# Weight halves by accumulating and casting DMA in the two gated MLPs of a hybrid decoder trunk

## The chip, the cores and the metric

The kernel runs on one core of a Trainium2 chip, written against the engines directly with a tile framework that orders each engine's instructions when the program is built. The metric is device time in microseconds of one launch. The kernel before takes 1498.43 us, the median of three runs (1496.72 to 1500.53).

## The reference, cut to what matters

Two layers over 528 tokens (16 learned ones and 512 of the sequence), model width 1024. Layer 0 is forgetting attention with 16 heads, layer 1 a gated linear recurrence with 8 heads; each is followed by the MLP that the change touches, with 2816 hidden columns:

```python
def conv_ffn(h, norm_g, w_gate, w_up, conv_w, conv_b, w_down):
    xn = rms_norm(h, norm_g)
    a = xn @ w_gate
    a_pad = jnp.pad(a, ((0, 0), (CONV_WIDTH - 1, 0), (0, 0)))
    a = (conv_b + conv_w[0] * a_pad[:, 0:L] + conv_w[1] * a_pad[:, 1:L + 1]
         + conv_w[2] * a_pad[:, 2:L + 2])
    return (jax.nn.silu(a) * (xn @ w_up)) @ w_down
```

All inputs and outputs are float32.

## The kernel before, in words

Activations lie transposed: 128 features by 528 tokens per tile, 8 such tiles for the width, 22 for the hidden columns. Products in float32 are built from three passes of TensorE in its reduced format (F32R). Each operand is split into hi, the value rounded to that format, and lo, what is left over; a product is hi·hi + hi·lo + lo·hi (`proj_unit`, L204, L207, L208). So every weight tile has to be split before use, and that is what `weights` does (L174 to L194), from three pools: `raw` with 2 buffers, `hi` and `lo` with 3 each. A tile is 128 x 1024 numbers (512 KB) or 128 x 896 (448 KB).

1. SyncE's queue issues the load of `raw` from HBM (L189). It can start when a raw buffer is free, that is when the split two tiles back has read it.
2. ScalarE casts `raw` to `hi` (L190), when TensorE has given up the hi buffer of three tiles back.
3. VectorE subtracts: `lo = raw - hi` (L191, recorded at the helper's line L122).

The run has six parts in a row: attention, first MLP (from 388 to 776 us of the profile), recurrence, and second MLP (from 1118 us to the end) are the four large ones, with output projections ahead of each MLP. An MLP (`ffn`) first writes the split activations `xhi`, `xlo` and the norm's factors `rsb`. Then it goes through the 22 hidden tiles m, called turns in what follows. A turn takes a gate weight tile, 24 matmuls for each half of the tokens, evicted by VectorE into `A` (L1048); the convolution of width three (L1050, L1053, L1056); a sigmoid on ScalarE (L1057); the up weight tile with its matmuls, multiplied in as they are evicted (L1062); and the split of the result into `ahi` (ScalarE, L1063) and `alo` (VectorE). In the first MLP GpSimd clears two columns of `A` each turn (L1046); the second starts at a later token and needs none. The down part then takes, for each of 8 output tiles, three weight tiles of 1024, 896 and 896 columns (22 blocks of 128), and VectorE adds the sum to the residual `h` (L1070). In the first MLP the tokens of a product go in two halves of 264 (`halves`, since 528 is more than a bank's 512): `unit` takes all weight tiles that it is given for the first half, then the same for the second. For gate and up that is one weight tile, used 24 + 24 times in a row. In the down part it is the three tiles of an output tile, one after the other, and then the same three again. In the second MLP the gate has two halves of 256 and 258 tokens, up and down one pass of 512.

Matmul sums go to the PSUM banks in rotation; the MLPs use six of them (`psp` 2, `pss` 4). The framework writes out the order of each engine at build time; each engine takes its own list strictly in that order, and waits at an instruction until what it needs is there.

Of the kernel before, what the change touches and what calls it, by code (L numbers as in the profile page):

```python
# [12 lines left out]
F32 = mybir.dt.float32  # L13
# [3 lines left out]
AF = mybir.ActivationFunctionType  # L17
ALU = mybir.AluOpType
# [3 lines left out]
P = 128  # L22
D = 1024
KT = D // P
# [50 lines left out]
def halves(t0):  # L75

    n = (T - t0) // 4 * 2
    return [(t0, n), (t0 + n, T - t0 - n)]


class Builder:
# [89 lines left out]
    def vcol(self, i):  # L171
        return self.vec[:, i : i + 1]

    def weights(self, src, n, w=P, parts=1):  # L174

        nc = self.nc
        raw = self.wraw.tile([P, 8 * P], F32, name="raw", tag="raw")[:, : n * w]
        hi = self.whi.tile([P, 8 * P], F32R, name="hi", tag="hi")[:, : n * w]
        lo = self.wlo.tile([P, 8 * P], F32R, name="lo", tag="lo")[:, : n * w]

        def load(c):
            nc.sync.dma_start(raw[:, c], src[:, c])
            nc.scalar.copy(hi[:, c], raw[:, c])
            self.sub(lo[:, c], raw[:, c], hi[:, c].bitcast(F32))

        self.raw = raw
        u = hi.rearrange("p (k c) -> p k c", c=w), lo.rearrange("p (k c) -> p k c", c=w), n
        if parts == 1:
            nc.sync.dma_start(raw, src)  # L189
            nc.scalar.copy(hi, raw)  # L190
            self.sub(lo, raw, hi.bitcast(F32))  # L191
            return u
        m = n * w // parts
        return *u, [partial(load, slice(i * m, i * m + m)) for i in range(parts)]  # L194
# [514 lines left out]
    def attend(self, o0, o1, p, ds, v, po, s2, maskk):  # L709
# [32 lines left out]
        for j in range(last + 1):  # L742
            w = []
            for hd in range(2):
                w.append(weights(hd, j))
                yield 0.25
            if due:
                values(due)
                yield 0.35 * len(due)
                due = []  # L750
            ready.append((j, w))
            if len(ready) == 2:
                due, ready = ready, []
# [265 lines left out]
    def ffn(self, ctx, layer, a0, o0):  # L1019

        nc, a = self.nc, self.a
        ga, up = (halves(t0) if T - t0 > 512 else [(t0, T - t0)] for t0 in (a0, o0))
        gcol, cw, cb = ((V_FFN0, V_CW0, V_CB0), (V_FFN1, V_CW1, V_CB1))[layer]
        sp = self.pool(f"ffn1_{layer}", 1, ctx=ctx)
        s2 = self.pool(f"ffn2_{layer}", 2, ctx=ctx)
        self.normsplit(gcol, a0)
        segs = (SEG0, SEG1)[layer]
        am, rs = self.token_stats(segs)
        self.spread_rs(rs, segs)
        def unit(w, toks, x):  # L1030
            for t0, tn in toks:
                ps = self.anybank()[:, :tn]
                for _ in self.proj_unit(ps, w, x, t0, tn):
                    pass
                yield ps, t0, tn

        ahi = sp.tile([P, NF, T - o0], F32R, name="ahi")
        alo = sp.tile([P, NF, T - o0], F32R, name="alo")
        ax = [(ahi[:, k, :], alo[:, k, :]) for k in range(NF)]
        n = T - o0  # L1040
        for m in range(NF):
            A = s2.tile([P, T + 2], F32, name="A", tag="A")
            t = s2.tile([P, T], F32, name="t", tag="t")
            s = s2.tile([P, T], F32, name="s", tag="sg")
            if o0 == 0:
                nc.gpsimd.memset(A[:, 0:2], 0.0)  # L1046
            for ps, t0, tn in unit([self.weights(a[f"gu{layer}"][m, 0], KT)], ga, self.x):
                nc.vector.tensor_tensor(A[:, 2 + t0 : 2 + t0 + tn], ps, self.rsb[:, t0 : t0 + tn], ALU.mult)  # L1048
            c0 = cw + 3 * m
            nc.vector.tensor_scalar(  # L1050
                t[:, :n], A[:, o0 + 2 : T + 2], self.vcol(c0 + 2), self.vcol(cb + m), ALU.mult, ALU.add
            )
            nc.vector.scalar_tensor_tensor(  # L1053
                t[:, :n], A[:, o0 + 1 : T + 1], self.vcol(c0 + 1), t[:, :n], ALU.mult, ALU.add
            )
            nc.vector.scalar_tensor_tensor(t[:, :n], A[:, o0:T], self.vcol(c0), t[:, :n], ALU.mult, ALU.add)  # L1056
            self.act(s[:, :n], t[:, :n], AF.Sigmoid)  # L1057
            nc.vector.tensor_tensor(t[:, :n], t[:, :n], s[:, :n], ALU.mult)
            nc.vector.tensor_tensor(t[:, :n], t[:, :n], self.rsb[:, o0:], ALU.mult)
            for ps, t0, tn in unit([self.weights(a[f"gu{layer}"][m, 1], KT)], up, self.x):  # L1060
                tv = t[:, t0 - o0 : t0 - o0 + tn]
                nc.vector.tensor_tensor(tv, ps, tv, ALU.mult)  # L1062
            nc.scalar.copy(ahi[:, m, :], t[:, :n])  # L1063
            self.sub(alo[:, m, :], t[:, :n], ahi[:, m, :].bitcast(F32))
        dn = [(t0 - o0, tn) for t0, tn in up]
        for m in range(KT):
            us = [self.weights(a[f"dn{layer}"][m][:, b * P : e * P], e - b) for b, e in ((0, 8), (8, 15), (15, 22))]
            for ps, t0, tn in unit(us, dn, ax):
                hv = self.h[:, m, o0 + t0 : o0 + t0 + tn]
                nc.vector.tensor_tensor(hv, ps, hv, ALU.add)  # L1070
                if layer == 1:
                    nc.sync.dma_start(a["out"][m][:, t0 : t0 + tn], hv)
            if layer == 0:
                self.sumsq(m)
# [99 lines left out]
```

## Time and profile before

| what | value |
|---|---|
| median of 3 runs | 1498.43 us (1496.72 to 1500.53) |
| profiled execution | 1497.61 us, span of its instructions 1495.8 us |
| TensorE (PE) busy | 1474.4 us, 99% |
| VectorE (DVE) busy | 892.8 us, 60% |
| ScalarE (ACT) busy | 524.9 us, 35% |
| GpSimd (POOL) busy | 32.3 us, 2% |
| HBM read | 116.10 MB |
| DMA queue q1 (issued by SyncE) | 131.57 MB, 29.1% of the 16 DMA engines' span |
| granted TensorE clock | 0.998 |

In the profile PE is TensorE, PEld its weight loads, DVE is VectorE, ACT ScalarE, POOL GpSimd, SP SyncE, and SPq the queue of DMAs that SyncE issues. `L190` is line 190 of the kernel. A matmul's record is longer than the distance to the next one, because matmuls are pipelined; time is read from distances and stretches, not from single matmuls.

### The profile page before, as it was taken

What the parts mean: (1) busy time and instruction counts of PE and PEld (TensorE: products, weight loads), DVE (VectorE), ACT (ScalarE), POOL (GpSimd) and SP (SyncE); (2) the same over time, 40 slices, a digit from 0 to 9 for tenths busy, and PEclk for the clock granted to TensorE, in tenths of its full rate; (3) what the DMA queues carried; (4) which work ended last, traced back from release to release, by engine and by line L of the source; (5) the groups of instructions that cost most, each with busy time, mean ns of one, the idle gap of its engine ahead of it and who ended that gap; (6) DMA issues with size and microseconds to landing.
All of it is one profiled execution on the core that took longest, in us unless ns stands there. A gap on an engine that the chain in (4) does not pass through costs nothing.

```text
span 1495.8 us, 27540 instructions
## 1 busy us (share of the span) xinstructions
PE 1474.4 (99%) x11352; PEld 1361.8 (91%) x11352; DVE 892.8 (60%) x1881; ACT 524.9 (35%) x1007; POOL 32.3 (2%) x113
## 2 busy tenths in 40 slices
PE   7999999999999999999999999999999999999999
PEld 6888888979999999999999989999999989988887
DVE  6555555775677667643335667676566667675221
ACT  5456555654233222222222333333342232222121
POOL 6000000000000000000000000000000000000000
PEclk9999999999999999999999999999999999999999
DMA  4433344413232322322322211211132232332331
GB/s 156 117 103 88 102 106 127 116 52 96 96 99 85 96 88 88 95 78 80 104 83 71 72 35 52 71 63 52 57 101 97 86 99 87 96 98 83 121 104 60
DMA packets 44821, 133.33 MB, mean 89 GB/s; under 512 B 7432, under 2 KB 7944, under 8 KB 44696
## 3 DMA queue, kind: packets, MB, share of 16 engines
q1 hardware_dynamic: 44696, 131.57, 29.1%
q8 instruction: 89, 1.46, 0.4%
q14 instruction: 36, 0.29, 0.1%
HBM read 116.10 MB, written 2.10 MB: 79 GB/s over the span
## 4 chain that ended last, share of the span: by engine, by line
PE 96%; DMA 2%; DVE 1%; SPq 1%; ACT 1%; issue 0%; DVEq 0%; ACTq 0%
PE pss L208 13%; PE pss L207 13%; PE pss L204 13%; PE psp L204 12%; PE psp L207 12%; PE psp L208 12%; PE psp L253 5%; PE psc L737 2%; PE pss L888 1%; PE pss L666 1%; PE pss L722 1%; PE pss L867 1%; PE pss L723 1%; DMA h<-h 1%; PE pss L963 1%; PE pss L894 1%
## 5 line engine op out<-in xcount | busy, mean ns | idle before, releaser
L190 ACT CAST hi<-raw 128x1024 fp32r<-128x1024 f32 (+2 forms) x218 | 221.8, 1018 | 569.4 <-PE pss L207 235.3
L122 DVE TENSOR_TENSOR lo<-raw,hi 128x1024 fp32r<-128x1024 f32 (+2 forms) x222 | 262.8, 1185 | 148.7 <-ACT hi L190 143.5
L204 PE MATMUL psp<-xhi,hi 128*128 128x264 f32 (+2 forms) x1160 | 332.9, 288 | 6.5 <-ACT xhi L273 6.5
L207 PE MATMUL psp<-xlo,hi 128*128 128x264 f32 (+2 forms) x1160 | 333.6, 288 | 3.4 <-DVE xlo L274 3.4
L208 PE MATMUL psp<-xhi,lo 128*128 128x264 f32 (+2 forms) x1160 | 332.7, 287 | 0.0
L208 PE MATMUL pss<-xhi,lo 128*128 128x264 f32 (+2 forms) x824 | 253.7, 308 | 0.0
L207 PE MATMUL pss<-xlo,hi 128*128 128x264 f32 (+2 forms) x824 | 253.0, 307 | 0.0
L204 PE MATMUL pss<-xhi,hi 128*128 128x264 f32 (+2 forms) x824 | 252.9, 307 | 0.0
L204 PEld LDWEIGHTS psp<-xhi,hi 128*128 128x128 f32 x1160 | 219.1, 189 | 11.1 <-ACT xhi L273 6.5
L207 PEld LDWEIGHTS psp<-xlo,hi 128*128 128x128 f32 x1160 | 219.5, 189 | 7.7 <-DVE xlo L274 4.1
L208 PEld LDWEIGHTS psp<-xhi,lo 128*128 128x128 f32 x1160 | 219.5, 189 | 1.2 <-issue 1.0
L204 PEld LDWEIGHTS pss<-xhi,hi 128*128 128x128 f32 x824 | 155.2, 188 | 7.8
L207 PEld LDWEIGHTS pss<-xlo,hi 128*128 128x128 f32 x824 | 155.0, 188 | 7.9
L208 PEld LDWEIGHTS pss<-xhi,lo 128*128 128x128 f32 x824 | 155.0, 188 | 7.7
L207 PE MATMUL pss<-alo,hi 128*128 128x264 f32 (+1 forms) x330 | 106.1, 322 | 0.0
L208 PE MATMUL pss<-ahi,lo 128*128 128x264 f32 (+1 forms) x330 | 106.0, 321 | 0.0
L204 PE MATMUL pss<-ahi,hi 128*128 128x264 f32 (+1 forms) x330 | 105.9, 321 | 0.0
L115 ACT ACTIVATE s<-t 128x528 f32<-128x528 f32 (+1 forms) x44 | 28.1, 639 | 121.6 <-DVE t L1056 121.6
L253 PE MATMUL psp<-hi,xhi 128*128 128x256 f32 x232 | 67.4, 290 | 2.7 <-ACT v L540 2.7
L208 PEld LDWEIGHTS pss<-ahi,lo 128*128 128x128 f32 x330 | 62.3, 189 | 4.9
L204 PEld LDWEIGHTS pss<-ahi,hi 128*128 128x128 f32 x330 | 62.1, 188 | 4.9
L253 PE MATMUL psp<-lo,xhi 128*128 128x256 f32 x232 | 66.5, 287 | 0.0
(405 smaller groups left out, 2603.3 us busy)
## 6 DMA issues: line engine op xcount, KB each, us to landing
raw<-gu SPq DMA_DIRECT2D x88, 512.0 KB
raw<-dn SPq DMA_DIRECT2D x32, 448.0 KB
pk<-stg SPq DMA_DIRECT2D x48, 264.0 KB
raw<-dn SPq DMA_DIRECT2D x16, 512.0 KB
raw<-wqk SPq DMA_DIRECT2D x14, 512.0 KB
raw<-wv SPq DMA_DIRECT2D x8, 512.0 KB
raw<-wg SPq DMA_DIRECT2D x8, 512.0 KB
raw<-hv SPq DMA_DIRECT2D x8, 512.0 KB
```

The lines of the kernel that those rows point to most:

```text
L115: ins = self.nc.scalar.activation(out, in_, func, **kw)
L122: self.nc.vector.tensor_tensor(out, x, y, ALU.subtract)
L190: nc.scalar.copy(hi, raw)
L204: ins = mm(ps, hi[:, i, :], xh, start=k == 0, stop=False)
L207: mm(ps, hi[:, i, :], xl, start=False, stop=False)
L208: mm(ps, lo[:, i, :], xh, start=False, stop=k == total - 1)
L253: mm(ps[:tn, :256], y[:, t0 : t0 + tn], w, start=n == 0, stop=n == 23)
L666: mm(o, q1[0:66, qs : qs + qn], k1[0:66, c0:c1], start=True, stop=False)
L722: self.score = mm(o, k1[0:98, ks : ks + kn], q1[0:98, q0:o1], start=True, stop=False)
L723: mm(o, k2[:, ks : ks + kn], q2[:, q0:o1], start=False, stop=True)
L737: ins = mm(o, v[:kn, j, 2 * (p % 2) + hd, :], w[hd][0], start=j == 0, stop=j == last)
L867: mm(pl[:, i, :, :], kp[:, t0 : t0 + tn], qk[:, t0 // 2 : (t0 + tn) // 2, :], start=True, stop=True)
```

## The change

`weights` gets a parameter `form`, set in `ffn` by the layer and by no other caller.

In the first MLP (`add`) ScalarE casts raw to hi as before, then writes `lo = -hi` with a second pass, and a transfer issued by GpSimd adds raw onto lo in SBUF (`accum_op=ALU.add`). VectorE's subtraction is gone there. The raw buffer is now read by that transfer, so it is free when the transfer has landed.

In the second MLP (`cast`) a transfer issued by GpSimd writes hi straight from HBM, converting float32 to F32R on the way; ScalarE's cast is gone there. Raw is still loaded from HBM by SyncE's queue, and VectorE still subtracts.

```diff
-    def weights(self, src, n, w=P, parts=1):
+    def weights(self, src, n, w=P, parts=1, form=None):
...
         if parts == 1:
             nc.sync.dma_start(raw, src)
-            nc.scalar.copy(hi, raw)
-            self.sub(lo, raw, hi.bitcast(F32))
+            if form == "cast":
+                nc.gpsimd.dma_start(hi, src)
+            else:
+                nc.scalar.copy(hi, raw)
+            if form == "add":
+                nc.scalar.activation(lo, hi.bitcast(F32), AF.Copy, scale=-1.0)
+                nc.gpsimd.dma_start(lo, raw, accum_op=ALU.add)
+            else:
+                self.sub(lo, raw, hi.bitcast(F32))
             return u
...
     def ffn(self, ctx, layer, a0, o0):
+        form = ("add", "cast")[layer]
...
-            for ps, t0, tn in unit([self.weights(a[f"gu{layer}"][m, 0], KT)], ga, self.x):
+            for ps, t0, tn in unit([self.weights(a[f"gu{layer}"][m, 0], KT, form=form)], ga, self.x):
...
-            for ps, t0, tn in unit([self.weights(a[f"gu{layer}"][m, 1], KT)], up, self.x):
+            for ps, t0, tn in unit([self.weights(a[f"gu{layer}"][m, 1], KT, form=form)], up, self.x):
...
-            us = [self.weights(a[f"dn{layer}"][m][:, b * P : e * P], e - b) for b, e in ((0, 8), (8, 15), (15, 22))]
+            us = [self.weights(a[f"dn{layer}"][m][:, b * P : e * P], e - b, form=form) for b, e in ((0, 8), (8, 15), (15, 22))]
```

The lines of the changed kernel are numbered anew: `weights` by up to seven more (the casting transfer is L192, the cast L194, the negation L196, the accumulating transfer L197), `ffn` by nine more.

ScalarE in the middle of the first MLP, before. The numbers behind the names tell buffers apart; each `hi` is one weight tile, gate and up in turn, and `s` is the sigmoid.

```order
L190 CAST hi_6156<-raw_6155 128x1024
L115 ACTIVATE s_5961<-t_5960 128x528
L190 CAST hi_6220<-raw_6219 128x1024
L1063 CAST ahi_5188<-t_5960 128x528
L190 CAST hi_6284<-raw_6283 128x1024
L115 ACTIVATE s_6089<-t_6088 128x528
```

The same place in the changed kernel:

```order
L115 ACTIVATE s_5973<-t_5972 128x528
L194 CAST hi_6236<-raw_6235 128x1024
L1072 CAST ahi_5188<-t_5972 128x528
L196 ACTIVATE lo_6237<-hi_6236 128x1024
L194 CAST hi_6301<-raw_6300 128x1024
L196 ACTIVATE lo_6302<-hi_6301 128x1024
```

Each cast into hi has got a negation behind it. For the tile whose cast comes after the sigmoid, a gate tile, `ahi` of the turn stands between the cast and its negation; for the other, an up tile, nothing does.

ScalarE in the down part of the first MLP, before: three weight tiles of an output tile, with the square and the split `xhi` for the next layer's norm.

```order
L190 CAST hi_8321<-raw_8320 128x1024
L190 CAST hi_8327<-raw_8326 128x896
L190 CAST hi_8333<-raw_8332 128x896
L266 ACTIVATE sq_8317<-h_58 128x528
L273 ACTIVATE xhi_100<-h_58,vec_59 128x528
```

and in the changed kernel:

```order
L194 CAST hi_8371<-raw_8370 128x1024
L196 ACTIVATE lo_8372<-hi_8371 128x1024
L194 CAST hi_8378<-raw_8377 128x896
L196 ACTIVATE lo_8379<-hi_8378 128x896
L274 ACTIVATE sq_8367<-h_58 128x528
L281 ACTIVATE xhi_100<-h_58,vec_59 128x528
L194 CAST hi_8385<-raw_8384 128x896
L196 ACTIVATE lo_8386<-hi_8385 128x896
```

Each cast has its negation right behind it, and the third tile now comes after the square and `xhi` instead of ahead of them.

GpSimd in the turns of the first MLP, before, did nothing but clear A:

```order
L1046 MEMSET A_6087 128x2
L1046 MEMSET A_6215 128x2
L1046 MEMSET A_6343 128x2
L1046 MEMSET A_6471 128x2
L1046 MEMSET A_6599 128x2
```

and in the changed kernel:

```order
L1055 MEMSET A_6231 128x2
L197 DMA lo_6237<-raw_6235 128x1024
L197 DMA lo_6302<-raw_6300 128x1024
L1055 MEMSET A_6361 128x2
L197 DMA lo_6367<-raw_6365 128x1024
L197 DMA lo_6432<-raw_6430 128x1024
```

Two accumulating transfers now stand between two clearings of A, one for a gate and one for an up tile.

GpSimd in the second MLP, where it had nothing to do before, now issues the casting transfers one behind the other:

```order
L192 DMA hi_13385<-gu1 128x1024
L192 DMA hi_13449<-gu1 128x1024
L192 DMA hi_13486<-gu1 128x1024
L192 DMA hi_13550<-gu1 128x1024
L192 DMA hi_13587<-gu1 128x1024
```

Nothing else stands on GpSimd's list from there to the end. SyncE's list of loads is the same in both kernels but for the line numbers. On TensorE a few matmuls of the norms' factors stand some places earlier at the start of each MLP; otherwise its order is the same but for the banks that some sums go to.

## Prediction

> **What bounds the kernel now.** I read the page first (busy shares, chain), then a table of stretches for the four parts of the two MLPs, then the waits and the order of time inside one turn of the first MLP, and last the DMA traffic in windows of a microsecond or so.
>
> ```profile
> span 1495.8 us, 27540 instructions
> PE 1474.4 (99%) x11352; PEld 1361.8 (91%) x11352; DVE 892.8 (60%) x1881; ACT 524.9 (35%) x1007; POOL 32.3 (2%) x113
> PE 96%; DMA 2%; DVE 1%; SPq 1%; ACT 1%; issue 0%; DVEq 0%; ACTq 0%
> ...
> 388.00:646.00 258.00, 258.00 (x2126) 258.00 (x2125) 179.32 (x278) 74.62 (x90) 2.12 (x22) 1.00 0.28 89
> 646.00:776.00 130.00, 130.00 (x1064) 130.00 (x1063) 44.89 (x57) 33.55 (x40) 0.00 (x0) 1.00 0.28 84
> 1124.00:1372.00 248.00, 248.00 (x1569) 224.06 (x1569) 174.10 (x256) 73.59 (x88) 0.00 (x0) 1.00 0.29 91
> 1372.00:1496.00 124.00, 120.21 (x518) 97.11 (x516) 29.43 (x30) 20.54 (x21) 0.00 (x0) 1.00 0.31 95
> ```
>
> The four long rows are stretches (length, then busy time of PE, PEld, DVE, ACT, POOL, then granted clock, DMA share, GB/s): gate and up of the first MLP, its down part, and the same two of the second. In three of them TensorE is busy for the whole stretch; in the fourth it lacks only the kernel's end. The clock is at 1.00. So taking work from VectorE or ScalarE, both far from full here, can give nothing. The change can only lose, and it loses where a weight tile comes later than TensorE wants it. The question is how much time a tile has.
>
> A turn of the first MLP is two weight tiles, gate and up:
>
> ```profile
> 501.27 1.05 ACT L190 CAST hi<-raw 128x1024 fp32r<-128x1024 f32 x1 [4.17 <-PE psp L207]
> 507.10 1.05 ACT L190 CAST hi<-raw 128x1024 fp32r<-128x1024 f32 x1 [1.36 <-PE pss L207]
> 508.13 0.64 ACT L1063 CAST ahi<-t 128x528 fp32r<-128x528 f32 x1
> 512.93 1.05 ACT L190 CAST hi<-raw 128x1024 fp32r<-128x1024 f32 x1 [4.16 <-PE pss L207]
> ...
> 501.81 0.55 DVE L1050 TENSOR_SCALAR t<-A,vec 128x528 f32<-128x528 f32 x1
> 502.35 1.23 DVE L122 TENSOR_TENSOR lo<-raw,hi 128x1024 fp32r<-128x1024 f32 x1
> ...
> 503.60 6.16 SPq L189 DMA_DIRECT2D raw<-gu  x2
> ...
> SPq L189 <- DVE lo L122: 212.2, 39, 7.4
> ACT hi L190 <- PE pss L207: 72.0, 28, 4.6
> ACT hi L190 <- PE psp L207: 31.6, 13, 4.2
> ```
>
> The turn is 512.93 - 501.27 = 11.66 us, a tile 5.83. The last three rows are waits between 400 and 640 us (who <- for whom: us in total, times, longest). There the cast into hi waits for TensorE to give up the buffer three tiles back (28 + 13 = 41 casts in 240 us, one per 5.83), not for its load. The load of the next but one raw tile waits for the subtraction (39 times, 212.2 us, 5.4 each of the 5.83). So the loop that can close is the one through the two raw buffers: load, split, and only then the load two tiles on. It must fit into one turn.
>
> ```profile
> 503.60:504.50 0.90, 0.90 (x10) 0.90 (x9) 0.86 (x2) 0.00 (x0) 0.00 (x0) 1.00 0.00 0
> 504.50:506.50 2.00, 2.00 (x19) 2.00 (x18) 1.27 (x2) 0.64 (x1) 0.10 (x1) 1.00 0.83 252
> 506.50:507.40 0.90, 0.90 (x10) 0.90 (x9) 0.78 (x2) 0.30 (x1) 0.00 (x0) 1.00 0.12 41
> ...
> 47.35 3.66 DMA raw<-wqk
> 51.03 1.05 ACT hi L190
> ...
> raw<-gu SPq DMA_DIRECT2D x88, 512.0 KB
> raw<-wqk SPq DMA_DIRECT2D x14, 512.0 KB
> raw<-dn SPq DMA_DIRECT2D x32, 448.0 KB
> ```
>
> The load issued at 503.60 moves nothing for 0.9 us, then traffic runs until about 507.4; where a load of that size stands on the chain of waits (third block), it counts 3.66 us and the cast follows at once. Today's loop of gate and up is 3.66 + 1.05 + 1.23 = 5.9 of 11.66 us: half the turn is spare.
>
> The down part of the first MLP is tighter, by its order of work: the three weight tiles of an output tile are gone through for the first half of the tokens and then all three again for the second, so each holds its hi and lo buffers until its second pass, and there are three buffers. One output tile there:
>
> ```profile
> 706.55 1.05 ACT L190 CAST hi<-raw 128x1024 fp32r<-128x1024 f32 x1 [7.61 <-PE pss L207]
> 709.15 0.94 ACT L190 CAST hi<-raw 128x896 fp32r<-128x896 f32 x1 [1.55 <-PE pss L207]
> 712.40 0.94 ACT L190 CAST hi<-raw 128x896 fp32r<-128x896 f32 x1 [2.31 <-DMA raw<-dn]
> 713.24 0.64 ACT L266 ACTIVATE sq<-h 128x528 f32<-128x528 f32 x1
> ...
> 722.71 1.05 ACT L190 CAST hi<-raw 128x1024 fp32r<-128x1024 f32 x1 [8.20 <-PE psp L207]
> ...
> 707.63 1.23 DVE L122 TENSOR_TENSOR lo<-raw,hi 128x1024 fp32r<-128x1024 f32 x1 [3.53 <-ACT hi L190]
> ```
>
> It takes 722.71 - 706.55 = 16.16 us, 0.367 for each of its 2 x 22 weight blocks. The third cast already waits for its load: the raw buffer came free with the subtraction of the first tile, at 708.86, and the cast follows 3.54 us later. So here both loops run in one: raw of the third tile hangs on the split of the first, and the split of the next first tile on TensorE's passage through the third.
>
> **The change, part by part: first MLP.** Removed: 68 subtractions on VectorE (1.23 us for 1024 columns), worth nothing since it has idle time there. Added on ScalarE: 68 passes lo = -hi. The trace has no such pass of 1024; by
>
> ```profile
> L273 ACT ACTIVATE xhi<-h,vec x32: 710/724/736, 5.7 to 1119.6; 128x528 fp32r<-128x528 f32 x24, 128x514 fp32r<-128x514 f32 x8
> ```
>
> a pass with a factor takes 0.72 against the 0.64 of ahi, a cast of the same 528 elements, so 0.08 more: 1.05 + 0.08 = 1.13 us for 1024, and 0.94 + 0.07 = 1.01 for 896. 68 of them, some 75 us, come to an engine that now works 108 of 388 us: no bound by themselves. But each stands in its tile's loop, and in ScalarE's new order the cast ahi (0.64) stands between the cast and the negation of each gate tile.
>
> Added on GpSimd: 68 accumulating transfers, lo += raw. Let La be the time from the end of the negation until one of 512 KB has landed. Raw is free only then, as the transfer reads it. GpSimd's memsets of A, which stand between, wait only for the convolution two turns back, and add nothing.
>
> No accumulating transfer is in the trace. From below, it is a load of the same size: 3.66. From above, every byte is read twice and written once in turn, 1.57 MB, at the rate of the nearest SBUF-to-SBUF traffic:
>
> ```profile
> 285.50 6.12 SPq L551 DMA_DIRECT2D pk<-stg  x6
> ...
> 287.50:290.50 3.00, 3.00 (x27) 2.94 (x26) 2.65 (x5) 1.15 (x6) 0.00 (x0) 1.00 0.98 199
> ```
>
> 199 GB/s with the DMA engines full (0.98): 7.9 us and the 0.9 ahead of it, 8.8. I take the middle case, two reads with the write alongside: 1.05 MB / 199 = 5.3, with 0.9 before, La = 6.2, and 0.9 + 0.92 / 199 = 5.5 for 448 KB. It is nearest to that row, the only one without the HBM in it. For being delayed by other transfers I add nothing: the HBM load reached 252 GB/s at a share of 0.83, so full engines with whole weight rows move more than 199, and that margin stands for the delay. Its bound is the load's own 0.28 x 5.83 = 1.6 us for each transfer in a loop.
>
> The Trainium skill ("DMA: Bandwidth & Descriptors", section "SDMA does more than copy") lists the add in a transfer as an elementwise reduction of two streams, which speaks for two reads; no run here shows it.
>
> Gate and up: the loop of a gate tile becomes 3.66 (load) + 1.05 (hi) + 0.64 (ahi) + 1.13 (-hi) + La = 6.48 + La against 11.66. Up to La = 5.18 it costs nothing; with 6.2 the turn is 12.68, 1.02 more. Of 22 turns one and a half run on tiles loaded ahead: 20.5 x 1.02 = 21 us.
>
> Down: the loop over one output tile is the third tile's load 3.54, cast 0.94, negation 1.01 and transfer 5.5; TensorE's first pass through it 7 x 0.367 = 2.57 and the second pass through the first tile 8 x 0.367 = 2.94; and then the next first tile's cast 1.05, negation 1.13 and transfer 6.2. Sum 24.9 us against 16.16, 8.7 more, seven times from one output tile to the next: 61 us. This loop is 13.3 + 1.875 La, so it is full at La = 1.5 already; at 3.66 it is 20.15, and the part loses 4.0 x 7 = 28 us. Only here does every reasonable La cost something.
>
> **Second MLP.** ScalarE loses 68 casts, worth nothing with TensorE full. The raw load stays, so the weights are read from HBM twice, once through the casting transfer on GpSimd's queue. That waits for TensorE to free hi; behind it stand only other such transfers. It lands between 3.66 us after issue (a load) and 6.6 (the 2.9 us of traffic from 504.5 to 507.4 doubled by the raw load beside it). VectorE's subtraction waits for it, so evictions queue behind that; but six PSUM banks of at least 248 / 88 = 2.8 us each stand between them and TensorE. The tile is ready at worst 6.6 + 0.77 (one VectorE operation in the way) + 1.23 = 8.6 us after the buffer came free. All tokens go in one pass in up and down there, so no tile is held for a second one, and the next use is two tiles on: 2 x 248 / 44 = 11.3, in the down part 2 x 120.2 / 24 = 10.0. Hidden: I take 0, with 1.4 us to spare. DMA share goes from 0.29 to some 0.6.
>
> The few matmuls of the norms that change place at the two MLPs' starts stay between others while TensorE has work: 0.
>
> **Sum.** 21 + 61 = +82 us. The profiled execution took 1497.61 (span 1495.8), 0.8 under the median 1498.43; 1498.4 + 82 = 1580 us. All of it hangs on La: around 6.2, each microsecond is 20.5 + 1.875 x 7 = 34 us. Low end, La 3.66: 0 + 28, 1526 us. High end, La 8.8 and 1.6 of delay on each transfer: a turn of 18.5, 6.8 over, x 20.5 = 140; an output tile of 29.8 + 4.9 = 34.7, 18.5 over, x 7 = 130; 1768 us.
>
> **Rivals.** (a) Not slower: raw, or the sum, is there within 1.5 us of the negation, 1498 us. Place: the down part's loop; it decides at La = 1.5, where 13.3 + 1.875 La passes 16.16. For it: gate and up have half a turn spare, and TensorE is never idle there now. Against: a plain load of this size moves nothing for 0.9 us and takes 3.66. Chance 0.05.
>
> (b) As quick as a load: the engines read both streams at once, La 3.7 to 4.5; gate and up hidden, the down part +28 to +40, 1526 to 1540 us. For it: loads use the engines to 0.28 only. Against: an add must read what it adds to. Chance 0.18.
>
> The Trainium skill's fit for a GpSimd transfer ("DMA: Bandwidth & Descriptors", "Anatomy of one DMA") is 2.0 us plus bytes over 436 GB/s, an estimate of 3.2 us here; by it the sum would be 3.1 x 7 = +22 us in the down part alone. The trace's plain load, at 3.66, is already longer than that.
>
> (c) Much slower: three passes, or transfers in each other's way; DMA share near 1 in the first MLP, over 1640 up to 1768 us. For it: 0.98 at only 199 GB/s in the SBUF-to-SBUF row. Against: the load's 252 at 0.83. Chance 0.17.
>
> (d) The second MLP pays too: the casting transfer needs over about 9 us (8.0 in the down part). At 10, 1 x 20.5 + 2 x 12 = +45 us on top, 1625 us. Against: HBM loads land in 3.66. Chance 0.03.
>
> (e) Faster: only if matmuls themselves ran closer together, for which no row speaks. 0.02. That the casting transfer does not replace the raw load is certain from the code; it alters no term.
>
> One rule would add to mine: the Trainium skill ("SBUF — State Buffer", "Who interferes with whom") says that VectorE in a two-port mode keeps GpSimd from writing a transfer's descriptors, and tensor_scalar is of a kind named there. By that rule, at most the 0.55 us of L1050 above would come on top of each turn, an estimate of 11 us in all; no run here shows it.
>
> **How the numbers follow.** My case, La 4.5 to 7.5, 1540 to 1640 us, 0.55; (a) 0.05; (b) 0.18; (c) 0.17; (d) 0.03; (e) 0.02. About 0.3% (4.5 us) is what a measurement of this kernel can tell from no change. Slower is 0.55 + 0.18 + 0.17 + 0.03 = 0.93, same 0.05, faster 0.02. The range runs from 1520, which takes (b) in, to 1690, above which lies about half of (c); below it lie (a) and (e).
>
> **What would show it.** Right: in the first MLP ScalarE's cast waits for the raw load instead of TensorE, SP's queue waits for the accumulating transfer, TensorE has gaps ahead of matmuls that read lo, most of them in the down part, where an output tile takes about 25 us; a turn of gate and up takes about 12.7; the second MLP keeps 248 and 124 us. The step that carries the sum is La = 6.2: a turn still at 11.66 with a slower down part makes (b) right, a turn of 15 or more (c). Gaps in the second MLP would make (d) right; a down part still at 130 us would overturn my loop.

## The result and the profile after

The changed kernel takes 1542.30 us (median of three runs, 1537.16 to 1542.36) against 1498.43 us: 1.0281 times as long, 95% interval 1.0251 to 1.0311, so 44 us slower. The forecast was 1580 us with a range of 1520 to 1690: right in sign, inside the range, 38 us too high. The profiled execution took 1542.36 us, with a span of 1540.6.

First the head of the page after: span, busy engines, shares of the chain that ended last.

```profile
span 1540.6 us, 27729 instructions
PE 1489.8 (97%) x11352; PEld 1370.2 (89%) x11352; DVE 817.5 (53%) x1813; ACT 520.4 (34%) x1007; POOL 129.0 (8%) x249
PE 70%; DMA 19%; issue 5%; ACT 4%; SPq 1%; DVE 1%; POOL 0%; POOLq 0%; ACTq 0%; DVEq 0%
```

TensorE was 96% of that chain and is 70% now, with transfers at 19%. The span grew by 44.8 us and TensorE's busy time by 15.4 for the same 11352 matmuls; the other 29 are idle time. The waits of the whole trace (who <- for whom: us in total, times, longest) say for what:

```profile
PE pss L216 <- DMA lo<-raw: 17.7, 17, 2.2
PE psp L216 <- DMA lo<-raw: 10.7, 10, 2.7
ACT hi L194 <- DMA raw<-gu: 131.5, 29, 7.4
```

TensorE's 17.7 + 10.7 = 28.4 us are all ahead of matmuls that read lo, waiting for the accumulating transfer. ScalarE's cast, which waited for TensorE before, now waits for the raw load, and in the waits of SyncE's own queue the load waits for the accumulating transfer, once for each of the 68 tiles:

```profile
SPq L190 <- DMA lo<-raw: 408.0, 68, 11.4
```

The parts' limits are read from three rows in each trace's order of time: the first matmul of the gate, the first one of the down part, and the first operation of the recurrence's gates. Before, then after:

```profile
388.02 0.29 PE L204 MATMUL pss<-xhi,hi 128*128 128x264 f32 x1
...
646.98 0.28 PE L204 MATMUL psp<-ahi,hi 128*128 128x264 f32 x1
...
776.90 0.13 DVE L787 TENSOR_TENSOR mx<-vec 128x8 f32<-128x8 f32 x1
```

```profile
391.05 0.29 PE L212 MATMUL pss<-xhi,hi 128*128 128x264 f32 x1
...
669.34 0.28 PE L212 MATMUL psp<-ahi,hi 128*128 128x264 f32 x1
...
821.85 0.13 DVE L795 TENSOR_TENSOR mx<-vec 128x8 f32<-128x8 f32 x1
```

Gate and up take 669.34 - 391.05 = 278.3 us instead of 259.0: 19.3 lost. The down part takes 152.5 instead of 129.9: 22.6. Together 41.9 of the 44.8. The other 3.0 were lost ahead of the gate's first matmul (391.05 against 388.02); three runs below whose time is that of the kernel before lost 1.1, 2.1 and 2.9 us there too, so they are no sign of the change. The table of stretches for the second MLP, 44 us later than in the prediction (columns as there), has the time and TensorE's share of before; ScalarE's busy time fell from 73.6 and 20.5 us, and the DMA share rose from 0.29 and 0.31:

```profile
1168.00:1416.00 248.00, 248.00 (x1569) 224.16 (x1570) 174.41 (x254) 26.93 (x43) 23.25 (x44) 1.00 0.57 182
1416.00:1540.00 124.00, 120.92 (x521) 97.75 (x519) 31.92 (x33) 0.62 (x1) 11.08 (x21) 1.00 0.59 183
```

In the middle of gate and up, the chain of waits in order of time (start, length, what) is a closed ring of two transfers and ScalarE:

```profile
529.09 4.55 DMA lo<-raw
...
533.69 4.55 DMA raw<-gu
...
538.31 2.83 issue
...
541.16 4.56 DMA lo<-raw
```

This turn is 541.16 - 529.09 = 12.07 us, against 11.66 before, and it is one of the shortest. Between the casts of these two gate tiles lie 17 turns, 12.86 us on average (12.0 to 15.3):

```profile
431.37 1.05 ACT L194 CAST hi<-raw 128x1024 fp32r<-128x1024 f32 x1 [3.96 <-DMA raw<-gu]
...
649.91 1.05 ACT L194 CAST hi<-raw 128x1024 fp32r<-128x1024 f32 x1 [6.10 <-DMA raw<-gu]
```

The 2.83 called issue are ScalarE's cast, `ahi` and negation, which the next rows show in the order of its time, up to the 0.28 between the negation's end and the transfer:

```profile
538.32 1.05 ACT L194 CAST hi<-raw 128x1024 fp32r<-128x1024 f32 x1 [6.05 <-DMA raw<-gu]
539.27 0.63 ACT L1072 CAST ahi<-t 128x528 fp32r<-128x528 f32 x1
539.80 1.05 ACT L196 ACTIVATE lo<-hi 128x1024 fp32r<-128x1024 f32 x1
```

In the quoted turn La is 0.28 + 4.55 = 4.8 us. Over all 68, issue to landing is longer:

```profile
DMA to landing us min/median/max: 4.2/5.7/8.3
```

**A correction.** The part on the change says that TensorE's order is otherwise the same but for banks. That is wrong for the down part of the first MLP. Let A, B, C be an output tile's three weight tiles and 1, 2 the two halves of the tokens; counted in blocks of 128 at the matmuls that read lo, TensorE's list for the second output tile is:

```
before:  A1 x8   B1 x7   C1 x7   A2 x8   B2 x7   C2 x7
after:   A1 x8   A2 x4   B1 x7   A2 x4   B2 x7   C1 x7   C2 x7
```

When the framework wrote out the order for the changed kernel, it mixed the two halves, so a tile's hi and lo buffers are given up much earlier. The mix is not the same for every output tile: from the third on, C1 stands between two parts of B2. One of the experiments puts the order of before back.

### The profile page after: what moved, and what is told of

It is laid out like the page before. It is cut to its first block, busy times and chain, and to the rows that moved or that the text cites. A ratio compares the mean times of both kernels' runs of the same rounds, so it can differ in the third digit from the quotient of the medians.

```text
span 1540.6 us, 27729 instructions
## 1 busy us (share of the span) xinstructions
PE 1489.8 (97%) x11352; PEld 1370.2 (89%) x11352; DVE 817.5 (53%) x1813; ACT 520.4 (34%) x1007; POOL 129.0 (8%) x249
## 4 chain that ended last, share of the span: by engine, by line
PE 70%; DMA 19%; issue 5%; ACT 4%; SPq 1%; DVE 1%; POOL 0%; POOLq 0%; ACTq 0%; DVEq 0%
PE psp L212 9%; PE psp L215 9%; PE psp L216 9%; DMA lo<-raw 8%; DMA raw<-gu 8%; PE pss L216 8%; PE pss L215 7%; PE pss L212 7%; PE psp L261 5%; PE psc L745 2%; DMA raw<-dn 2%; ACT lo L196 2%; PE pss L896 1%; ACT hi L194 1%; PE pss L730 1%
## 5 line engine op out<-in xcount | busy, mean ns | idle before, releaser
L194 ACT CAST hi<-raw 128x1024 fp32r<-128x1024 f32 (+2 forms) x150 | 151.9, 1014 | 400.6 <-DMA raw<-gu 131.5
L122 DVE TENSOR_TENSOR lo<-raw,hi 128x1024 fp32r<-128x1024 f32 (+2 forms) x154 | 181.7, 1182 | 159.3 <-DMA hi<-dn 59.2
L216 PEld LDWEIGHTS pss<-xhi,lo 128*128 128x128 f32 x824 | 155.8, 189 | 18.1 <-DMA lo<-raw 10.4
L197 POOL DMA_DIRECT2D lo<-raw x68 | 59.5, 875 | 444.2 <-ACT lo L196 343.1
L122 DVE TENSOR_TENSOR alo<-t,ahi 128x528 fp32r<-128x528 f32 (+1 forms) x44 | 30.8, 700 | 117.2 <-ACT ahi L1072 117.2
L196 ACT ACTIVATE lo<-hi 128x1024 fp32r<-128x1024 f32 (+1 forms) x68 | 70.2, 1033 | 1.4
```

The costliest lines, as they stand in the source:

```text
L122: self.nc.vector.tensor_tensor(out, x, y, ALU.subtract)
L196: nc.scalar.activation(lo, hi.bitcast(F32), AF.Copy, scale=-1.0)
L197: nc.gpsimd.dma_start(lo, raw, accum_op=ALU.add)
L216: mm(ps, lo[:, i, :], xh, start=False, stop=k == total - 1)
```

## The experiments

Each is the changed kernel with one edit, run beside the kernel before on the same chip (medians of before 1498.05, 1498.27 and 1498.45 us). Losses of gate and up, and of the down part, are read from the same three rows as above, in the profiled execution, which can lie some us off the median.

**The two parts of the change, each alone.** First the accumulating form in the first MLP only:

```diff
-        form = ("add", "cast")[layer]
+        form = ("add", None)[layer]
```

> The first MLP as in the changed kernel, the second as before. Theory L (the loop through the two raw buffers of the first MLP - load, cast, negation, accumulating transfer, next load - sets the time there, and the casting transfers of the second MLP are hidden): 1537 to 1543 us, the whole loss. Rival C (the casting transfers take part of the loss, by queueing or by DMA traffic): less than 1530.

Measured: 1541.14 us, ratio 1.0291 (1.0275 to 1.0307): the changed kernel's loss. Then the casting form in the second MLP only:

```diff
-        form = ("add", "cast")[layer]
+        form = (None, "cast")[layer]
```

> The first MLP as before, the second as in the changed kernel. Theory L: the same as the kernel before, 1496 to 1501 us, ratio within 0.997 to 1.003. Rival C: 1505 us or more, with TensorE gaps in the second MLP.

Measured: 1498.38 us, ratio 1.0003 (0.9994 to 1.0012). The casting transfer is hidden, and the whole loss is the first MLP's.

**A third raw buffer** in the first MLP, every third tile from a pool of its own:

```diff
-        raw = self.wraw.tile(
+        third = form == "add" and self.nadd % 3 == 2
+        self.nadd += form == "add"
+        raw = (self.wraw3 if third else self.wraw).tile(
```

> The changed kernel with a third raw buffer in the first MLP (two from the old pool and one from a pool of its own), so that a load waits for the accumulating transfer three tiles back instead of two. The same bytes are moved. Theory L: three tiles are there for a loop of some 12 us where 17.5 are needed by TensorE, so gate and up fall back to 11.66 us a turn and the total to 1498 to 1508 us (in the down part the hi and lo buffers may still leave some). Rival B (bandwidth: the DMA engines, at a share of 0.7 in the first MLP, are what is short): no change, 1535 to 1545 us.

Measured: 1505.69 us, ratio 1.0052 (1.0032 to 1.0072). The stretches of gate and up and of the down part with what follows:

```profile
388.00:660.00 272.00, 271.45 (x2234) 271.11 (x2233) 134.96 (x238) 120.95 (x137) 41.87 (x68) 1.00 0.78 180
660.00:840.00 180.00, 174.27 (x1411) 168.32 (x1410) 51.23 (x124) 67.52 (x83) 19.79 (x33) 1.00 0.57 140
```

TensorE is full in the first, at a higher DMA share (0.78) than the 0.71 which the changed kernel has between 388 and 669 us. The transfers are no shorter (4.2/5.9/8.0), so it is neither their length nor their traffic that costs time there, but that the loop runs through two raw buffers. Gate and up lose nothing (258.9 us) where they lost 19.3, the down part 8.1 instead of 22.6. The order of the down part is mixed here nearly as in the changed kernel (from the second output tile on C1 comes after one or two blocks of B2 there).

**TensorE's order of before** forced in the down part of the first MLP: the first matmul of each half waits in the list for the last one of the half before.

```diff
-                mm(ps, lo[:, i, :], xh, start=False, stop=k == total - 1)
+                self.endmm = mm(ps, lo[:, i, :], xh, start=False, stop=k == total - 1)
...
-        def unit(w, toks, x):
+        def unit(w, toks, x, chain=False):
...
-                for _ in self.proj_unit(ps, w, x, t0, tn):
+                for _ in self.proj_unit(ps, w, x, t0, tn, self.endmm if chain else None):
...
-            for ps, t0, tn in unit(us, dn, ax):
+            for ps, t0, tn in unit(us, dn, ax, layer == 0):
```

> The changed kernel with TensorE's order in the down part of the first MLP as the kernel before had it: all three weight tiles for the first half of the tokens, then all three for the second. Theory O (the prediction's loop over an output tile was right for that order, and the built program got around it by mixing the two halves): the down part costs 13.3 + 1.875 La with La of 4.9 to 5.8, that is 22.5 to 24.2 us an output tile instead of 18.5, 7 x 4 to 5.7 more, total 1566 to 1582 us. Rival R (the raw buffers' loop alone sets the down part, whatever TensorE's order): 1537 to 1545 us.

Measured: 1590.62 us, ratio 1.0618 (1.059 to 1.0645): 48 us more than with the mixed order, and 9 over the theory's range. The down part takes 201.6 us, 49 more than with the mixed order (gate and up, with 18.1 us of loss, 1 less). ScalarE's casts of the first weight tile of two output tiles in a row, in its order of time:

```profile
736.89 1.05 ACT L194 CAST hi<-raw 128x1024 fp32r<-128x1024 f32 x1 [12.71 <-PE pss L215]
...
761.85 1.05 ACT L194 CAST hi<-raw 128x1024 fp32r<-128x1024 f32 x1 [11.83 <-PE pss L215]
```

They are 24.96 us apart where the prediction had 24.9; the mean of all seven such distances is 25.5, over the 24.2 at which the theory's range ended. So the loop that the prediction described is real; the changed kernel does not run it, because its order is another.

**How long the transfer is, and what it holds.** Four runs. In the first the transfer copies, so nothing is subtracted and lo holds raw; TensorE's order is that of the changed kernel, matmul for matmul:

```diff
-                nc.gpsimd.dma_start(lo, raw, accum_op=ALU.add)
+                nc.gpsimd.dma_start(lo, raw)
```

> The transfer on GpSimd's queue copies raw to lo without adding, so lo holds raw instead of raw - hi; passes, waits and queues are those of the changed kernel. Theory (a loop through two raw buffers; the second read that the add needs makes the transfer long): it lands in 3.2 to 3.7 us instead of 5.7, the gate and up loop fits into its 11.66 us, and the time is 1498 to 1510 us. Rival (most of the transfer is fixed cost, so an add takes no longer than a copy): it lands in 5 us or more and the time stays at 1530 to 1545 us.

Measured: 1499.50 us, ratio 1.0002 (0.999 to 1.0013). Issue to landing of the 68 copies:

```profile
DMA to landing us min/median/max: 2.7/2.9/4.9
```

A copy of the same bytes between the same buffers lands in half the time of the sum, and the kernel loses nothing. GpSimd's queue in the changed kernel and in this run (packets, MB, share of the 16 engines' span; the second MLP's casting transfers are in both):

```profile
q0 software_dynamic: 19584, 69.21, 19.8%
q0 software_dynamic: 19584, 69.21, 14.3%
```

Packets and bytes are the same, in 305 and 214 us of each engine's time. The adding transfers alone, in the run with the first MLP's part of the change, took 12.4% of 1538.9 us, 191; so the copies take about 100, and a packet of the sum is about twice as long. The add makes the transfer long, as two reads instead of one would; the trace does not show the reads themselves.

In the second the transfer adds the weights from HBM instead of from raw:

```diff
-                nc.gpsimd.dma_start(lo, raw, accum_op=ALU.add)
+                nc.gpsimd.dma_start(lo, src, accum_op=ALU.add)
```

> The accumulating transfer takes the weights from HBM a second time instead of from raw, so raw is free again as soon as ScalarE's cast has read it. Theory (the loss is the raw buffer held through the transfer): SyncE's queue waits for the cast instead of the transfer, and the time is 1498 to 1512 us although 34 MB more are read from HBM. Rival (the loss is traffic, or lo coming late by itself whatever raw does): 1535 us or more.

Measured: 1531.80 us, ratio 1.0224 (1.0209 to 1.0239), far over the theory's 1512. Half of it holds: gate and up are back (no loss, TensorE full from 388 to 660 us), with raw free after the cast and 34.6 MB more read. The down part lost 32.1 us, 9.5 more than in the changed kernel. Its order had moved too: A1 x8, A2 x6, B1 x7, A2 x1, C1 x7, A2 x1, B2 x7, C2 x7, with the last block of A2 only after C1, almost the order of before. The edit was not the single change that it was meant to be; the next run is its counterpart with a known order.

**Third raw buffer and the order of before,** the two edits above together:

> A third raw buffer in the first MLP, and in its down part TensorE's order of before (three weight tiles for the first half of the tokens, then again for the second). Theory (two loops, one through the raw buffers, one through the hi and lo buffers): gate and up are back at their time of before, and of the down part only the piece remains in which the next output tile's first weight tile must be split after TensorE gives up its buffer: cast 1.05, negation 1.06, transfer 5 to 6 = 7.4 to 8.4 us where 2.57 + 2.57 of TensorE's passes cover it, some 2.3 to 3.3 us for each of 7 output tiles, 1514 to 1530 us. Rival (the order alone sets the down part's time): 24.5 us for each output tile as with the order of before and two raw buffers, so 1555 us or more.

Measured: 1532.64 us, ratio 1.0235 (1.0218 to 1.0252), 2.6 us over the theory's range, far from the rival's. Gate and up are back (no loss); the down part takes 162.6, 32.7 more, the same as in the run before. Without the raw loop, hi and lo held through both halves cost that much. ScalarE's first casts of two output tiles are 20.4 us apart there (745.74 and 766.13), 4.2 more than 16.16 where 2.3 to 3.3 were expected; in that stretch the accumulating transfers on the chain of waits take 6.4 to 6.7 us, where 5 to 6 had been put in.

**A microsecond more in the loop:** ScalarE writes the negation twice.

```diff
                 nc.scalar.activation(lo, hi.bitcast(F32), AF.Copy, scale=-1.0)
+                nc.scalar.activation(lo, hi.bitcast(F32), AF.Copy, scale=-1.0)
```

> ScalarE writes the negation twice, one behind the other, in the first MLP: 1.06 us more between cast and transfer of each weight tile, nothing else. Theory (a loop of latencies through the raw buffers): each turn of gate and up gets longer by 1.06 x 20.5 = 22 us in all, the down part by up to 12 x 1.06 = 13 us: 1565 to 1580 us. Rival (the transfers' traffic sets the pace, ScalarE's time is slack): 1537 to 1548 us.

Measured: 1563.60 us, ratio 1.0426 (1.0376 to 1.0475), 21 over the changed kernel and just under the theory's range. In the profiled execution, the slowest of the four (1569.20 us), gate and up lose 42.8 us, 23.5 more than with one negation, against 22 expected. The down part takes 158.1 us, 5.6 more where up to 13 were expected; its order is again a different mix. Work on an engine that is busy a third of the time costs its full length where it stands in the closed loop.

**Each weight tile for both halves in a row.** The down part of the first MLP is written out as A1 A2 B1 B2 C1 C2, for three raw buffers and for two:

```diff
+        def both(us, x):
+            pss = [self.anybank()[:, :tn] for t0, tn in dn]
...
+            for hi, lo, n in us:
+                for ps, (t0, tn) in zip(pss, dn):
+                    for i in range(n):
...
-            for ps, t0, tn in unit(us, dn, ax):
+            for ps, t0, tn in both(us, ax) if layer == 0 else unit(us, dn, ax):
```

> A third raw buffer in the first MLP, and in its down part TensorE uses each weight tile for both halves of the tokens in a row, so its hi and lo buffers are held for one pair of passes only. Theory (two loops, one through two raw buffers, one through three hi and lo buffers, and nothing else): both are open, TensorE waits for no transfer, 1496 to 1502 us; the accumulating transfers are then free though no shorter. Rival (the transfers' length or traffic keeps a cost of its own): 1505 us or more, as with the third raw buffer alone.

Measured with three: 1497.85 us, ratio 0.9993 (0.9983 to 1.0002). The stretches:

```profile
388.00:660.00 272.00, 272.00 (x2242) 272.00 (x2241) 134.91 (x238) 123.00 (x139) 42.52 (x69) 1.00 0.79 181
660.00:840.00 180.00, 180.00 (x1518) 175.03 (x1518) 55.12 (x132) 69.85 (x92) 19.02 (x33) 1.00 0.57 138
```

TensorE is full in both, although the transfers land as late as ever (median 5.8 us). That is the whole cost of the change, accounted for: with both loops open it costs nothing. It brings nothing either, since TensorE was the bound before.

> TensorE's order as in the run with the third raw buffer (each weight tile of the down part for both halves in a row), but two raw buffers as in the changed kernel. Theory: gate and up keep their whole loss of 22 us; in the down part only the loop through the raw buffers is left, where two tiles take about 12.1 less the 0.64 of ahi, 11.5 us, so three take 17.2 instead of 16.16, some 7 us in all: 1520 to 1533 us. Rival (in the down part the raw buffers cost nothing and the order alone did): 1515 to 1522 us; rival (the order has no part in it): 1538 us or more.

Measured with two: 1533.88 us, ratio 1.0229 (1.0199 to 1.0258), 0.9 us over the theory's range by the time, and wrong inside: in the profiled execution (1538.14 us) the down part lost 20.4 us, not 7. The chain of waits there:

```profile
697.72 5.46 DMA lo<-raw
703.19 0.02 SPq L190
...
703.24 3.85 DMA raw<-dn
...
708.02 0.64 ACT sq L274
708.66 0.62 ACT xhi L281
709.28 3.43 DMA raw<-dn
...
715.22 7.42 DMA lo<-raw
722.64 0.02 SPq L190
...
722.69 4.77 DMA raw<-dn
```

The ring of gate and up again, now with the norm's square and `xhi` between cast and negation, once for each output tile, and transfers of 5.46 and 7.42 us. So in the down part, too, the raw loop alone costs nearly what the changed kernel loses there.

The times in us by TensorE's order in the down part and by raw buffers:

| order of the down part | two raw buffers | three |
|---|---|---|
| as before: A1 B1 C1 A2 B2 C2 | 1590.6 | 1532.6 |
| mixed by the framework (not quite alike) | 1542.3 (the change) | 1505.7 |
| each tile for both halves | 1533.9 | 1497.9 |

## Why the prediction was right, and where it was wrong

**TensorE bounds, so the change can only lose:** right. The first MLP's subtraction, gone from VectorE, brought nothing in any run.

**The second MLP, 0:** right, and by itself 1.0003. The casting transfer lands in 3.4/4.2/6.3 us (shortest, median, longest), where 3.66 to 6.6 were put in. Rival (d) falls.

**Gate and up, 21 us:** measured 19.3. The loop is the one described, shown by the third raw buffer (the loss goes) and by the second negation (23.5 us more), and a turn is 12.86 where 12.68 was forecast. The size came out through errors that cancel. In the mean of the 17 turns between the two quoted casts, La of the gate tile is 5.4 (6.2 was put in), cast, `ahi` and negation are 2.5 together (2.8), and from the transfer's landing to the next gate tile's cast, which is the next load, pass 4.9 (3.66). By the prediction's own formula 6.48 + 5.4 = 11.9 would have been 0.2 over the turn of before, some 4 us in all. The delay of the load, for which it added nothing, makes the rest of the loss; that other transfers cause the delay is likely but not shown by a run of its own.

**Down part, 61 us:** measured 22.6. This is the step that failed. It rested on TensorE taking the three tiles for the first half and all three again for the second, and in the changed kernel it does not. Where that order was forced, the loop took 24.96 us against the 24.9 of the sum, and the whole kernel 1590.6 us. Its terms, from the chain of waits of that run, show what cancels in that output tile:

```profile
739.32 4.55 DMA lo<-raw
...
743.92 4.09 DMA raw<-dn
...
748.09 0.95 ACT hi L194
...
750.02 0.28 issue
```

and TensorE after its wait for the third tile's lo, in its order of time:

```profile
754.57 0.59 PE L216 MATMUL psp<-ahi,lo 128*128 128x264 f32 x1 [4.92 <-DMA lo<-raw]
```

The first tile's transfer is 4.55 (with its 0.28, 4.8 instead of 6.2). The third tile's load takes 4.09 and its cast follows at 748.09, 4.2 instead of 3.54. Its lo lands at 754.57, where TensorE starts, 4.55 after its negation ended at 750.02, where 5.5 had been put in. From there to the next first cast are 7.3 us instead of 2.57 + 2.94 = 5.5, since TensorE runs slower after its wait (last section). In sum -1.4 + 0.7 - 1.0 + 1.8, near nothing. That the total came out inside the range is owed to the range's width and not to this term.

**La = 6.2** was close. Counted from the end of the negation, as the prediction does, the 68 transfers land after 4.5 to 8.6 us, 5.9 on average. Of its two bounds, the load's 3.66 lies under the shortest, and the 8.8 just over the longest. The idea behind it, a second read, fits the copy, which lands in 2.9 us from issue. The fit of the Trainium skill ("DMA: Bandwidth & Descriptors", "Anatomy of one DMA"), an estimate of 3.2 us here, is near that copy and not near the sum, with its 5.7.

**Rivals.** (a), not slower, did not come; a transfer of 2.9 us gives it, and so do open loops with transfers of 5.8. (b), as quick as a load with 1526 to 1540, lies nearest in time and is not what happened: it had gate and up hidden and all of the loss in the down part. (c) does not hold, with a DMA share of 0.71. Of the tests that the prediction named, ScalarE waiting for the raw load and SyncE's queue for the transfer came out, and so did a turn of about 12.7. TensorE's gaps lie in the down part by time (15.8 of 28.4 us), not by number (12 of 27), and an output tile there took some 19 us, not 25.

The estimate from the Trainium skill ("SBUF — State Buffer", "Who interferes with whom"), 11 us for VectorE holding up GpSimd, has no run of its own here. With both loops open nothing of that size shows in the time.

## What to carry to other kernels

A transfer that replaces an engine's pass lengthens the time for which its source is held, so count the loop through each buffer pool before the busy shares: one more buffer, together with the order in which the consumer gives buffers up, was worth all of the 44 us here, and the engine relieved was worth none. Where a framework writes out the order, read the consumer's new order at the place of every large term, since a change in a producer can move it; here that step would have shown that the term of 61 us had no ground. A sum that fits may hold errors that cancel, so measure the terms too.

## What the runs showed of the hardware

After some waits of about two microseconds TensorE ran at half its pace for longer than the wait. In the changed kernel, from TensorE's order of time:

```profile
776.98 0.39 PE L216 MATMUL pss<-ahi,lo 128*128 128x264 f32 x1 [1.78 <-DMA lo<-raw]
777.21 0.28 PE L212 MATMUL pss<-ahi,hi 128*128 128x264 f32 x1
...
777.73 0.42 PE L215 MATMUL pss<-alo,hi 128*128 128x264 f32 x1
777.95 0.42 PE L216 MATMUL pss<-ahi,lo 128*128 128x264 f32 x1
```

The matmuls are 0.12 us apart at first, then 0.22 for some 3.4 us, then 0.12 again. In the first MLP of this kernel it followed 3 of 27 gaps (1.78, 2.20 and 2.73 us), but not another of 1.79, and it cost about 3 x 3.4 x (1 - 0.12 / 0.22) = 4.6 us, a part of the 15.4 that TensorE's busy time grew by; the rest was not taken apart. What decides is where a gap falls. The granted clock changes only on a fixed grid of 3.41 us. Two steps of that grid, each with the one behind it (columns as in the prediction):

```profile
774.23:777.64 3.41, 1.63 (x13) 1.42 (x13) 0.00 (x0) 2.10 (x2) 0.38 (x1) 1.00 0.54 106
777.64:781.06 3.42, 3.42 (x18) 3.42 (x18) 0.01 (x1) 0.00 (x0) 0.48 (x1) 0.50 0.95 220
...
709.38:712.79 3.41, 1.85 (x15) 1.86 (x16) 1.40 (x2) 1.06 (x2) 0.45 (x1) 1.00 0.78 135
712.79:716.20 3.41, 3.41 (x30) 3.41 (x30) 0.00 (x0) 1.22 (x2) 0.00 (x0) 1.00 0.81 249
```

The gap of 1.78 us lies within one step, and the next step has a clock of 0.50. The gap of 1.79 is spread over two, with 1.56 us (3.41 - 1.85) in the second, and the next keeps 1.00. In the twelve traces, from 350 us on, all 31 steps at full clock in which TensorE sat idle for over 1.80 us were followed by one at half clock, two of the four with 1.78 to 1.80, and none of the 65 with 1.00 to 1.75. Ahead of that, among the attention's matmuls, less was enough (1.2 us idle before 74.5 us in the changed kernel), so the figure holds for the matmuls from there on.

With the order of before forced, gaps of up to 5.4 us brought the granted clock to 0.88 between 660 and 840 us, where it was 1.00 with the third raw buffer. The Trainium skill ("TensorE: Matmul & The Clock Gate", Part 1, "What's actually happening") names a free-running window of about 3.4 us, and puts the half clock behind an idle one. The grid of 3.41 us agrees with that window; here 1.8 us of idling within it were enough.

An accumulating transfer of 512 KB or 448 KB within SBUF took 5.7 us in the median, a plain copy of the same tiles 2.9.
